# Moving matmul operands by 32 bytes in SBUF: stationary operands 32 bytes behind the moving ones, modulo 128

## The chip, the cores and the metric

The kernel runs on one core of one Trainium2 chip. The metric is the device time of one execution in microseconds. TensorE (PE) does the matmuls; a weight load (PEld, LDWEIGHTS) brings the stationary operand into the array, and the matmul then streams the moving operand past it. VectorE (DVE), ScalarE (ACT) and GpSimd (POOL) do the elementwise work, and SyncE (SP) issues most of the DMAs. SBUF is the on-chip memory; a tile's address is its byte offset within a partition.

## The reference

One decoder layer on a sequence of 2048 tokens and a model width of 1024, all in float32:

```python
def reference(x, ...):
    h = _rms(x, norm_mix_g[l])
    x = x + _mixer(h, ...)            # z = h @ w_in + b_in, three kinds of heads, y @ w_out
    h = _rms(x, norm_ffn_g[l])
    x = x + _conv_glu(h, ...)
    return x

def _conv_glu(h, w_up, conv_w, conv_b, w_down):
    u = _causal_dwconv(h @ w_up, conv_w) + conv_b
    gate, up = jnp.split(u, 2, axis=-1)
    return (jax.nn.silu(gate) * up) @ w_down
```

The mixer splits z into columns for eight attention heads with a forget gate, four mLSTM heads and four HGRN2 heads. w_in is 1024 x 3600, w_up 1024 x 5632, w_down 2816 x 1024.

## The kernel before

Every large product is done three times over in float32r: each operand is split into a high part and the rest, and high x high, high x rest and rest x high are summed in PSUM (`mm3`, L161). A split is a ScalarE copy and a subtraction on GpSimd or VectorE.

**Stages.** First the input projection, in two halves of 1024 tokens. `z_norm` (L169) normalises and transposes x into `hhi` and `hlo`, 128 partitions of the contraction, eight steps (`DT`) of 512 tokens. `z_groups` (L184) then walks through 14 groups of 256 columns of w_in. `load_split` (L146) loads a group's weights and splits them into `whi` and `wlo`. In a `ct_group` (L194) the weights are stationary and 512 tokens of `hhi`/`hlo` move, so that the result comes out transposed. In a `nat_group` (L207) 128 tokens of `hhi`/`hlo` are stationary and the weights move, 256 columns wide, or 264 in the two gated groups, where gate columns ride along. The moving weights of contraction step i begin at `whi[:, i, :]`, so i times 1024 bytes into the tile, or i times 1056 in the gated groups. The second half's groups are merged with the recurrent mixers. Then comes attention (L771 to L799), the output projection (`phase_out`, L877) and the feed-forward part.

**Feed-forward.** The up projection (`ffn_up`, L1048) runs for each half of the tokens over 22 pairs of column blocks. It uses a Strassen form with seven products instead of eight 512-deep ones: each product streams a 512-wide block of the tokens (`b11`, `b21`, `b22` or a sum or difference `t1` to `t4`, each as high part `h` and rest `l`) past a 128 x 128 block of the weights or of sums of them (tiles `w`). These weights come from the pool `fw`, but for three blocks of the first pair, which `up_first` puts into `hpool` ahead of time. `t3` and `b22` lie in the pool `ffnx2`, the other token blocks in `ffnx`. The down projection (`ffn_down`, L1164) is of the same form with both operands in `fw`.

**Addresses.** Pools are stacked from the left end of SBUF upwards or, with `side="right"`, from the right end downwards, in the order in which they are opened, so an unused tile at the right place shifts all that is opened after it. Four such tiles exist: `pad` (32 bytes) among the constants on the left, `padr` (32 bytes) first on the right, `padz` (32 bytes) in the pool of the input projection, and `padf` (256 bytes) in `ffnx`. With them the moving and the stationary operand of each matmul of the up, down, output and ungated input projections begin at the same address modulo 128 (64, in all of these).

The order of instructions is set by a scheduler when the kernel is built, except in the down projection, where it is written out.

Of the kernel before, what the change touches and what calls it, by code (L numbers as in the profile page):

```python
# [9 lines left out]
F32 = mybir.dt.float32  # L10
F32R = mybir.dt.float32r
# [9 lines left out]
P = 128  # L21
T = 2048
D = 1024
DT = D // P
# [118 lines left out]
        nc.vector.tensor_tensor(lo[:, 4 * q : 4 * q + 4, tok : tok + P], ps, h.bitcast(F32), op=ALU.subtract)  # L143


def load_split(k, wp, src, tag="w", n=2):  # L146

    nc = k.nc
    width = src.shape[1]
    hi = k.t(wp, [P, DT, width], F32R, tag=tag + "hi")  # L150
    lo = k.t(wp, [P, DT, width], F32R, tag=tag + "lo")
    for q in range(0, DT, n):
        raw = k.t(wp, [P, n, width], tag=tag + "raw")
        nc.sync.dma_start(raw, src[q * P : (q + n) * P, :].rearrange("(dt p) c -> p dt c", p=P))
        h = hi[:, q : q + n, :]
        nc.scalar.activation(h, raw, AF.Copy)  # L156
        nc.gpsimd.tensor_tensor(lo[:, q : q + n, :], raw, h.bitcast(F32), op=ALU.subtract)  # L157
    return hi, lo


def mm3(nc, out, lhs, rhs, n, lsl, rsl):  # L161


    for i in range(n):
        for j, (a, b) in enumerate(((0, 0), (0, 1), (1, 0))):
            nc.tensor.matmul(out, lsl(lhs[a], i), rsl(rhs[b], i), start=(i == 0 and j == 0), stop=(i == n - 1 and j == 2))  # L166
# [17 lines left out]
def z_groups(k, hf, pz, wp, psum, xbufs):  # L184
# [4 lines left out]
    w_in, b_in = k.a["w_in"][0], k.a["b_in"][0]  # L189
# [3 lines left out]

    def ct_group(off, dst, r0, c):  # L194

        w = load_split(k, wp, w_in[:, off : off + 256], n=4)
        for b in range(2):
            for ct in range(2):
                ps = k.t(psum, [P, BLK], tag="w")
                mm3(nc, ps, w, hts[b], DT, lambda x, i: x[:, i, ct * P : (ct + 1) * P], lambda x, i: x[:, i, :])  # L200
                st = k.t(pz, [P, BLK], tag="z", bufs=3)
                nc.scalar.activation(st, ps, AF.Identity, bias=k.col[:, c + ct : c + ct + 1])
                t0 = hf * HALF + b * BLK
                nc.scalar.dma_start(dst[r0 + ct * P : r0 + (ct + 1) * P, t0 : t0 + BLK], st)
                yield ct == 1
# [733 lines left out]
def h_tiles(k, fx, names):  # L939
    for n in names.split():  # L940
        k.hp[n] = tuple(fx.tile([P, 4, BLK], F32R, tag=n + x, name=n + x) for x in "hl")
# [378 lines left out]
def merge(main, side, rate):  # L1320

    due = 0.0
    for _ in main:
        due += rate
        while due >= 1.0:
            due -= 1.0
            if next(side, False) is False:
                due = 0.0
                break


def _trunk(ctx, tc, a, out):
    nc = tc.nc
    k = K(ctx, tc, a, out)

    def pool(stack, name, bufs, **kw):
        if kw.get("space") is not DRAM:
            kw["reuse_waits"] = "tile"
        return stack.enter_context(tc.tile_pool(name=name, bufs=bufs, **kw))

    dp = pool(ctx, "scratch", 1, space=DRAM)
    for name, shape in (
        ("s_qh", [512, T]),
        ("s_ql", [512, T]),
        ("s_kh", [512, T]),
        ("s_kl", [512, T]),
        ("s_v", [T, AH, 130]),
        ("s_fc", [AH, 2, T]),
        ("s_bqk", [512, T]),
        ("s_c", [512, T]),  # L1350
        ("s_n", [T, 1024]),
        ("s_rows", [NBLK, 28, BLK]),
        ("s_x2", [T, 1024]),
        ("s_h", [2, 2, 2, P, 4, BLK]),
        ("s_g", [2, 7, NP // 2, P, BLK]),
        ("s_w", [4, NP // 2, P, BLK]),
        ("s_one", [10, T]),
        ("s_y", [T, 1024]),
    ):
        setattr(k, name, dp.tile(shape, F32, tag=name, name=name))  # L1360
    cp = pool(ctx, "const", 1)
    k.ident = cp.tile([P, P], F32, tag="ident", name="ident")
    nc.scalar.dma_start(k.ident, a["ident"])
    k.halo = cp.tile([P, 2 * NP, 2], F32, tag="halo", name="halo")
    k.fcol = cp.tile([P, 4, 2 * NP], F32, tag="fcol", name="fcol")

    cp.tile([P, 8], F32, tag="pad", name="pad")
    pool(ctx, "pad", 1, side="right").tile([P, 8], F32, tag="padr", name="padr")

    with ExitStack() as ms:  # L1370
        cm = pool(ms, "cmix", 1)

        def mconst(name, shape, dt=F32, src=None):
            t = cm.tile(list(shape), dt, tag=name, name=name)
            if src is not None:
                nc.sync.dma_start(t, src)
            return t

        bc = ExitStack()
        pb = pool(bc, "bc", 1, side="right")  # L1380
        psb = pool(bc, "psb", 3, space=PSUM, side="right")
        k.q2 = pb.tile([P, 4, 2, P], F32, tag="q2", name="q2")
        nc.gpsimd.memset(k.q2, 0.0)
        with ExitStack() as zs:
            pz = pool(zs, "z", 2)
            wp = pool(zs, "w", 2)
            psw = pool(zs, "psw", 3, space=PSUM)
            k.gmix = pz.tile([P, D], F32, tag="gmix", name="gmix", bufs=1)
            xb, xw = ((pb, "v", 2), (pb, "p4", 2)), ((wp, "wraw", 2),)
            z = z_groups(k, 0, pz, wp, psw, (xb, xb))  # L1390
            next(z)
            pz.tile([P, 8], F32, tag="padz", name="padz", bufs=1)
            state(k, mconst)
            for _ in range(ZC):
                next(z)
            consts(k, a, cp, mconst, pz, psw, cm)
            mix = mixers(k, pb, psb)
            for _ in z:
                pass
            merge(z_groups(k, 1, pz, wp, psw, (xb, xw)), mix, RZ)  # L1400
        with ExitStack() as at:

            k.pat = {n: pool(at, "at_" + n, 1) for n in ("ga", "oT", "B0", "B1", "A0", "A1", "V1", "o1")}
            pa = pool(at, "att", 2)
            k.pat.update((n, pool(at, "at_" + n, 1)) for n in ("o0", "V0"))
            psa = pool(at, "psa", 2, space=PSUM)
            k.ga = k.pat["ga"].tile([P, 512], F32, tag="ga", name="ga", bufs=1)
            nc.sync.dma_start(k.ga, a["out_g"][0:1, 0:512].broadcast_to([P, 512]))
            att = attention(k, pa, psa)
            for _ in mix:  # L1410
                for _ in range(RA):
                    next(att, None)
            bc.close()
            wo = ExitStack()
            wor = ExitStack()
            w = w_out_load(k, pool(wo, "wo", 1, side="right"), pool(wor, "wor", 1, side="right"))
            for _ in att:
                pass

    wor.close()  # L1420
    py = pool(wo, "y", 2, side="right")
    psy = pool(wo, "psy", 1, space=PSUM, side="right")
    fx = pool(ctx, "ffnx", 1)

    fx.tile([P, 64], F32, tag="padf", name="padf")
    k.hp = {}
    h_tiles(k, fx, "b11 b21 t1 t2 t4")
    k.hpool = pool(ctx, "hpool", 10)
    with ExitStack() as os_:
        po = pool(os_, "po", 2)  # L1430
        k.gffn = po.tile([P, D], F32, tag="gffn", name="gffn", bufs=1)
        nc.sync.dma_start(k.gffn, a["norm_ffn_g"][0:1, :].broadcast_to([P, D]))
        pst = pool(os_, "pst", 2, space=PSUM)
        pso = pool(os_, "pso", 2, space=PSUM)
        psz = pool(os_, "psz", 1, space=PSUM)
        phase_out(k, w, py, (psy, psz), po, (psy, pso), pst)
    wo.close()
    fw = pool(ctx, "fw", 23, side="right")
    fx2 = pool(ctx, "ffnx2", 1, side="right")
    h_tiles(k, fx2, "t3 b22")  # L1440

    psp = [pool(ctx, f"psp{i}", 1, space=PSUM) for i in range(4)]
    k.psp = [psp[i] for i in (2, 3, 1, 0)]
    first = up_first(k)()
    h_parts(k, 0, 1)
    for hf in range(2):
        ffn_up(k, hf, fw, first)
        first = ffn_down(k, hf, fw)
# [19 lines left out]
def state(k, mconst):  # L1468

    nc = k.nc  # L1470
    k.half = mconst("half", [P, 1])
    nc.vector.memset(k.half, 0.5)

    sc = mconst("scan", [36, BLK])
    k.scan1 = k.scanc = sc
    nc.vector.memset(sc, 1.0)
    nc.vector.memset(sc.rearrange("p (c l) -> p c l", l=P)[32:36, :, 0:1], 0.0)
    k.carry = mconst("carry", [AH, 3])
    nc.vector.memset(k.carry, 0.0)
    nc.vector.memset(k.carry[:, 2:3], NEG)  # L1480
    k.bstate = mconst("bstate", [P, 2, 2, 65])
    nc.vector.memset(k.bstate, 0.0)
    k.cstate = mconst("cstate", [P, 2, HD])
    nc.vector.memset(k.cstate, 0.0)
# [105 lines left out]
```

## Time and profile before

| | us |
|---|---|
| median of 3 runs | 2980.77 (2980.37 to 2982.65) |
| profiled execution, its own time | 2982.74 |
| its span, first to last instruction | 2981.0 |
| PE busy | 2834.5 (95%) |
| PE weight loads busy | 2350.0 (79%) |
| DVE / ACT / POOL busy | 2055.0 / 1255.0 / 1412.5 |
| mean granted PE clock | 0.975 of full speed |

A group's line in the profile gives the source line, the engine, the operation, the tiles written and read, the shape, the number of instructions, their busy time in us, the mean of one in ns, and the idle time before them. A matmul's busy time runs on while the next one has already begun, so how fast a stream goes is read from the starts on the timeline and not from the length of one matmul: in the up projection a matmul is 389 ns long, and the next begins 227 ns after it. Matmul rows name the moving operand first and the stationary one second, and the weight load's rows are a group of their own (PEld).

### The profile page before, as it was taken

The page shows a single profiled execution, that of the slowest core. Times are in us where ns is not written, and L with a number is a line of the kernel's source. Part 1 is how long each engine was busy: PE and PEld are TensorE (multiplying, and loading weights), DVE is VectorE, ACT ScalarE, POOL GpSimd, SP SyncE. Part 2 cuts the span into 40 slices and gives each one's busy share as a digit, 9 for nine tenths or more (in the row PEclk, how much of TensorE's full clock was granted, in tenths as well). Part 3 has the DMA queues.
Part 4 walks back from the last instruction along what each step waited for, and adds up shares of the span by engine and source line. Part 5 has one row for each costly group of instructions (what it writes and reads, how often), then busy time and mean ns, then how long its engine had stood idle before and what let it go on. Part 6 is the DMA issues. An engine that isn't in the chain of part 4 may idle for free. (4 is left out here: it accounts for less than half of the span.)

```text
span 2981.0 us, 43125 instructions
## 1 busy us (share of the span) xinstructions
PE 2834.5 (95%) x15181; PEld 2350.0 (79%) x15181; DVE 2055.0 (69%) x3637; ACT 1255.0 (42%) x2138; POOL 1412.5 (47%) x1149
## 2 busy tenths in 40 slices
PE   7999999899978988899999999999999999999999
PEld 7889989899766665566688778888878888888887
DVE  6426688757379886777746567777697677777655
ACT  3232332312225456677623344444454344444443
POOL 2233434643245556756501176666476544444443
PEclk9999999999988889999999999999999999999999
DMA  5333434433261334433056634544677433333666
GB/s 170 115 113 123 148 106 128 144 93 94 93 149 49 77 66 97 100 71 66 18 182 212 198 129 163 161 157 155 222 263 260 155 105 105 100 102 124 226 206 214
DMA packets 332025, 406.88 MB, mean 136 GB/s; under 512 B 31010, under 2 KB 219504, under 8 KB 328640
## 3 DMA queue, kind: packets, MB, share of 16 engines
q1 hardware_dynamic: 296192, 335.37, 37.5%
q10 hardware_dynamic: 33264, 60.37, 5.4%
q0 software_dynamic: 2352, 8.39, 1.0%
q8 instruction: 119, 1.95, 0.3%
q14 instruction: 98, 0.80, 0.1%
HBM read 276.05 MB, written 127.98 MB: 136 GB/s over the span
## 5 line engine op out<-in xcount | busy, mean ns | idle before, releaser
L1027 POOL TENSOR_TENSOR w<-w,w 128x512 fp32r<-128x512 f32 x302 | 405.0, 1354 | 400.2 <-ACT w L1026 286.1
L1215 PE MATMUL ps<-w,w 128*128 128x512 f32 x1848 | 421.2, 390 | 4.4 <-ACT w L1206 1.9
L1215 PEld LDWEIGHTS ps<-w,w 128*128 128x128 f32 x1848 | 346.6, 188 | 78.2 <-POOL w L1208 2.6
L166 PE MATMUL w<-whi,hhi 128*128 128x256 f32 (+1 forms) x1280 | 369.4, 289 | 2.1 <-DVE pg L228 1.5
L166 PE MATMUL w<-wlo,hhi 128*128 128x256 f32 (+1 forms) x1280 | 367.7, 288 | 0.6 <-POOL wlo L157 0.6
L166 PE MATMUL w<-whi,hlo 128*128 128x256 f32 (+1 forms) x1280 | 367.0, 287 | 0.0
L783 POOL TENSOR_TENSOR pl<-pf,ph 128x512 fp32r<-128x512 f32 (+1 forms) x224 | 269.3, 1214 | 175.6 <-ACT ph L780 113.0
L1208 POOL TENSOR_TENSOR w<-w,w 128x512 fp32r<-128x512 f32 x154 | 215.4, 1405 | 204.4 <-ACT w L1206 172.3
L1026 ACT ACTIVATE w<-w 128x512 fp32r<-128x512 f32 x302 | 180.7, 627 | 261.0 <-POOL w L1027 82.5
L1207 DVE TENSOR_TENSOR w<-w,w 128x512 fp32r<-128x512 f32 x154 | 180.5, 1182 | 104.7 <-ACT w L1205 103.2
L166 PEld LDWEIGHTS w<-whi,hhi 128*128 128x128 f32 x1280 | 246.9, 193 | 3.7 <-issue 2.0
L166 PEld LDWEIGHTS w<-wlo,hhi 128*128 128x128 f32 x1280 | 246.7, 193 | 1.8 <-POOL wlo L157 1.0
L166 PEld LDWEIGHTS w<-whi,hlo 128*128 128x128 f32 x1280 | 246.4, 193 | 0.2
L745 DVE TENSOR_REDUCE mx<-m 128x1 f32<-128x512 f32 (+2 forms) x320 | 188.3, 604 | 63.6 <-PE m L740 36.2
L778 ACT ACTIVATE pf<-s 128x512 f32<-128x512 f32 (+1 forms) x320 | 168.4, 539 | 144.1 <-DVE pl L783 49.9
L157 POOL TENSOR_TENSOR wlo<-wraw,whi 128x1024 fp32r<-128x1024 f32 (+1 forms) x56 | 137.9, 2483 | 170.6 <-ACT whi L156 167.7
L1032 DVE TENSOR_TENSOR w<-w,w 128x512 f32<-128x512 f32 x176 | 151.2, 878 | 81.5 <-DMA w<-in_w_up_dram 69.4
L780 ACT ACTIVATE ph<-pf 128x512 fp32r<-128x512 f32 (+1 forms) x320 | 178.1, 575 | 45.8 <-PE pv L798 38.5
L1073 DVE SCALAR_TENSOR_TENSOR u<-ps,fcol,u 128x1023 f32<-128x1023 f32 x88 | 108.9, 1278 | 91.6 <-ACT u L1072 91.6
L771 PE MATMUL s<-QB,KB 70*128 70x512 f32 (+1 forms) x320 | 134.1, 419 | 30.7 <-ACT pf L778 30.3
L740 PE MATMUL m<-KB,QB 70*128 70x512 f32 (+2 forms) x320 | 135.3, 438 | 21.1 <-DVE mx L745 12.4
L1206 ACT ACTIVATE w<-w 128x512 fp32r<-128x512 f32 x154 | 96.7, 628 | 114.3 <-PE ps L1215 89.5
(349 smaller groups left out, 7102.1 us busy)
## 6 DMA issues: line engine op xcount, KB each, us to landing
w<-in_w_up_dram SPq DMA_DIRECT2D x182, 256.0 KB
w<-s_g SPq DMA_DIRECT2D x154, 256.0 KB
w<-in_w_down_dram SPq DMA_DIRECT2D x110, 256.0 KB
wraw<-in_w_in_dram SPq DMA_DIRECT2D x48, 512.0 KB
s_g<-u ACTq DMA_DIRECT2D x88, 256.0 KB
w<-s_w SPq DMA_DIRECT2D x88, 256.0 KB
s_g<-w ACTq DMA_DIRECT2D x66, 256.0 KB
w<-s_h SPq DMA_DIRECT2D x48, 256.0 KB
```

The source lines that it names most:

```text
L157: nc.gpsimd.tensor_tensor(lo[:, q : q + n, :], raw, h.bitcast(F32), op=ALU.subtract)
L166: nc.tensor.matmul(out, lsl(lhs[a], i), rsl(rhs[b], i), start=(i == 0 and j == 0), stop=(i == n - 1 and j == 2))
L745: nc.vector.tensor_reduce(mx[:, i, kb : kb + 1], ps[:, 0:n], axis=AX.X, op=ALU.max)
L778: nc.scalar.activation(pf[:, c0:], ps[:, c0:], AF.Exp)
L780: nc.scalar.activation(ph[:, c0:], pf[:, c0:], AF.Copy)
L783: eng.tensor_tensor(pl[:, c0:], pf[:, c0:], ph[:, c0:].bitcast(F32), op=ALU.subtract)
L1026: nc.scalar.activation(h, t, AF.Copy)
L1027: nc.gpsimd.tensor_tensor(lo, t, h.bitcast(F32), op=ALU.subtract)
L1032: nc.vector.tensor_tensor(t, x, y, op=op)
L1207: nc.vector.tensor_tensor(gl, gr, gh.bitcast(F32), op=ALU.subtract)
L1208: nc.gpsimd.tensor_tensor(wl, wr, wh.bitcast(F32), op=ALU.subtract)
L1215: nc.tensor.matmul(tiles[tile], g[x][:, tile * P : (tile + 1) * P], w[y], start=j == 0 and c == 0, stop=j == nj - 1 and c == 2,)
```

## The change

The change only moves tiles in SBUF. `pad` and `padz` go, `padr` grows from 32 to 64 bytes, `padf` shrinks from 256 to 224, and `load_split` gets a parameter `off`, a number of float32 elements left free at the front of `whi` and `wlo`; `ct_group` passes 16 (64 bytes).

```diff
-def load_split(k, wp, src, tag="w", n=2):
+def load_split(k, wp, src, tag="w", n=2, off=0):
...
-    hi = k.t(wp, [P, DT, width], F32R, tag=tag + "hi")
-    lo = k.t(wp, [P, DT, width], F32R, tag=tag + "lo")
+    hi, lo = (
+        k.t(wp, [P, off + DT * width], F32R, tag=tag + x)[:, off:].rearrange("p (a c) -> p a c", c=width)
+        for x in ("hi", "lo")
+    )
...
-        w = load_split(k, wp, w_in[:, off : off + 256], n=4)
+        w = load_split(k, wp, w_in[:, off : off + 256], n=4, off=16)
...
-
-    cp.tile([P, 8], F32, tag="pad", name="pad")
-    pool(ctx, "pad", 1, side="right").tile([P, 8], F32, tag="padr", name="padr")
+    pool(ctx, "pad", 1, side="right").tile([P, 16], F32, tag="padr", name="padr")
...
-            pz.tile([P, 8], F32, tag="padz", name="padz", bufs=1)
...
-    fx.tile([P, 64], F32, tag="padf", name="padf")
+    fx.tile([P, 56], F32, tag="padf", name="padf")
```

The addresses modulo 128 that follow, worked out from the tiles' places in the built program, and the offset stationary minus moving:

| matmuls | stationary, moving before | offset | stationary, moving after | offset |
|---|---|---|---|---|
| input, nat groups, 256 wide | `hhi` 64, `whi` 64 | 0 | `hhi` 32, `whi` 0 | 32 |
| input, gated nat groups, 264 wide | `hhi` 64, `whi` 64 + 32i | 0, 96, 64, 32 in turn | `hhi` 32, `whi` 32i | 32, 0, 96, 64 in turn |
| input, ct groups, 512 wide | `whi` 64, `hhi` 64 | 0 | `whi` 64, `hhi` 32 | 32 |
| up, with b11, b21, t1, t2, t4 | `w` 64, `b11` 64 | 0 | `w` 32, `b11` 0 | 32 |
| up, first pair's blocks from `hpool` | 64, 64 | 0 | 0, 0 | 0 |
| up, with t3, b22 | 64, 64 | 0 | 32, 32 | 0 |
| down | 64, 64 | 0 | 32, 32 | 0 |

The output projection and attention keep their offsets; the transposes get other ones. All offsets of 32 are 32 modulo 256, too. The order of the instructions on each engine is the same before and after. One thing beside addresses differs: `t3`'s high part now begins 32 bytes lower against the output stage's pool and so reaches 32 bytes into its second `x2` buffer, and ScalarE's first write to it waits for that buffer as well.

## The prediction

> **What bounds the kernel now.** I read the page's busy line and clock line first, then the chain, then the busy time by stage, then single matmuls on the timeline. The page:
>
> ```profile
> PE 2834.5 (95%) x15181; PEld 2350.0 (79%) x15181; DVE 2055.0 (69%) x3637; ACT 1255.0 (42%) x2138; POOL 1412.5 (47%) x1149
> PE ps L1058 25%; PE ps L1215 12%; PE w L166 1%; DMA w<-in_w_up_dram 1%; POOL w L1027 1%; DVE w L1032 1%; DVE u L1074 0%; POOL w L1208 0%; DVE w L965 0%; DMA w<-in_w_down_dram 0%; DVE u L1073 0%; DMA s_g<-w 0%; DMA w<-s_g 0%; PE tn L911 0%; ACT u L1072 0%
> ```
>
> TensorE is the bound, and in the part of the chain that the page follows the up projection (L1058) is the largest piece. The chain does not reach back to the input projection, so that stage has to be judged by its busy time. Stages below, as us, PE, PEld, DVE, ACT, POOL, clock, DMA: the two halves of the input projection (the second with the mixers beside it), attention, and the long stretches of the up projection in each half.
>
> ```profile
> 0.00:409.00 409.00, 384.60 (x2760) 363.02 (x2761) 235.44 (x642) 132.35 (x195) 127.90 (x123) 0.99 0.41 132
> 409.00:821.00 412.00, 393.83 (x2849) 364.92 (x2850) 274.02 (x640) 118.28 (x193) 168.34 (x165) 0.99 0.35 109
> 821.00:1480.00 659.00, 580.19 (x2985) 405.42 (x2984) 515.72 (x997) 381.66 (x746) 386.99 (x322) 0.91 0.35 78
> 1738.00:2123.00 385.00, 384.50 (x1696) 317.84 (x1695) 273.96 (x320) 167.96 (x266) 246.94 (x183) 1.00 0.49 161
> 2377.00:2760.00 383.00, 381.96 (x1681) 315.25 (x1682) 299.58 (x402) 157.67 (x219) 175.19 (x136) 1.00 0.33 106
> ```
>
> PE is busy 94% and 96% of the two input stages and over 99% of the up stretches, at full clock. So what counts is how far apart two matmuls start. One 512-wide and one 256-wide stream from the timeline (start us, length us), and a piece of the 256-wide stream in a window that the windows view gives as clock 0.50:
>
> ```profile
> 32.40:34.00 1.60, 1.60 (x9) 1.60 (x9) 1.56 (x5) 0.58 (x1) 0.00 (x0) 0.50 0.05 13
> ```
>
> ```profile
> 32.37 0.42 PE L166 MATMUL w<-wlo,hhi 128*128 128x256 f32 x1
> 34.08 0.41 PE L166 MATMUL w<-whi,hhi 128*128 128x256 f32 x1
> ...
> 38.74 0.28 PE L166 MATMUL w<-wlo,hhi 128*128 128x256 f32 x1
> 40.18 0.28 PE L166 MATMUL w<-wlo,hhi 128*128 128x256 f32 x1
> ...
> 1800.97 0.39 PE L1058 MATMUL ps<-t2h,w 128*128 128x512 f32 x1
> 1803.69 0.39 PE L1058 MATMUL ps<-t4h,w 128*128 128x512 f32 x1
> ```
>
> At half clock eight starts lie in 1.71 us, 214 ns for 256 columns; at full clock the columns alone would then take 107 ns, and 512 columns 213 ns. At full clock twelve 256-wide starts take 1.44 us (120.0 ns each), and twelve 512-wide ones 2.72 us (226.7 ns each). Both lose the same 13.3 ns per matmul over their columns, so the loss goes with the matmul, or with its weight load, and not with the columns. That loss is all that placement can touch.
>
> **The change part by part.** The instructions stand in the same order on every engine before and after; what differs are addresses. I count by the two addresses of each matmul, stationary minus moving, modulo 128 bytes. Before, the offset is 0 in the up projection, in the input projection's 256-wide and 512-wide groups, in the down projection and in the output projection. After, it is 32 in the 3,072 256-wide matmuls (1,024 of each of three kinds), in the 768 512-wide ones of the transposed groups (256 of each kind), and in 2,568 of the 3,696 of the up projection: 1,056 with t3 or b22 stay at 0, and so do 72 of the first column block, whose weights lie in another pool (3,696 − 1,056 − 72). Groups by form:
>
> ```profile
> L166 PE MATMUL w<-whi,hhi 128*128 128x256 f32 x1024 | 295.3, 289 | 0.6 <-ACT hhi L142 0.6
> L166 PE MATMUL w<-hhi,whi 128*128 128x512 f32 x256 | 101.8, 398 | 1.2 <-ACT z L202 1.2
> L1058 PE MATMUL ps<-b11h,w 128*128 128x512 f32 x352 | 117.0, 393 | 2.2 <-DVE u L1079 1.5 <-ACT halo L1076 0.5
> L1215 PE MATMUL ps<-w,w 128*128 128x512 f32 x1848 | 421.2, 390 | 4.4 <-ACT w L1206 1.9 <-POOL w L1208 1.5 <-ACT halo L1076 1.0
> ```
>
> So 6,408 matmuls are touched. On the path I count the 2,568 of the up projection whole, and nine tenths of the 3,840 of the input projection (PE's 94% and 96% there, less some for the mixers that share the stage): 3,456; together 6,024. Each nanosecond is 6.0 us, and 0.2% of the time, about the least that a measurement of this kernel can tell from no change, is 6 us: one nanosecond per matmul.
>
> The price of offset 32 stands nowhere as a steady stream, but the gated groups bound it. Their weight rows are 264 columns, 1,056 bytes, so the moving address steps 32 bytes modulo 128 with each of the eight contraction steps while the stationary one stays. The offset runs 0, 96, 64, 32, 0, 96, 64, 32 over steps of three matmuls. Starts of the first matmul of each step, one whole cycle:
>
> ```profile
> 105.73 0.28 PE L166 MATMUL w<-whi,hhi 128*128 128x264 f32 x1
> ...
> 106.09 0.28 PE L166 MATMUL w<-whi,hhi 128*128 128x264 f32 x1
> ...
> 106.45 0.29 PE L166 MATMUL w<-whi,hhi 128*128 128x264 f32 x1
> ...
> 106.82 0.28 PE L166 MATMUL w<-whi,hhi 128*128 128x264 f32 x1
> ...
> 107.17 0.28 PE L166 MATMUL w<-whi,hhi 128*128 128x264 f32 x1
> ...
> 107.53 0.28 PE L166 MATMUL w<-whi,hhi 128*128 128x264 f32 x1
> ...
> 107.90 0.28 PE L166 MATMUL w<-whi,hhi 128*128 128x264 f32 x1
> ...
> 108.26 0.29 PE L166 MATMUL w<-whi,hhi 128*128 128x264 f32 x1
> ...
> 108.63 0.28 PE L166 MATMUL w<-whi,hhi 128*128 128x264 f32 x1
> ```
>
> 264 columns are 110 ns by the same rate, 0.33 us a step. The steps take 0.36, 0.36, 0.37, 0.35, 0.36, 0.37, 0.36, 0.37 us. The two steps at offset 32 are the shortest and one of the longest: losses of 6.7 and 13.3 ns per matmul. The two at offset 0 lose 10 ns each, less than the steady 13.3 at the same offset, so three matmuls are too few to settle, and these rows give bounds rather than a price. The whole cycle is 2.90 us, 120.8 ns each, a loss of 10.8. That is the value I take for a steady offset 32, as the mean over all offsets, since the two direct readings lie on either side of it (mean 10.0). The saving is 13.3 − 10.8 = 2.5 ns; 6,024 × 2.5 ns = 15.1 us.
>
> The ends: the best step (6.7) saves 6.6 ns, 40 us; losing nothing at all would save 13.3 ns, 80 us. Upwards, a 512-wide stream at offset 0 that has just been interrupted runs slower before it settles:
>
> ```profile
> 1738.84 0.40 PE L1058 MATMUL ps<-t3h,w 128*128 128x512 f32 x1
> ...
> 1740.00 0.62 PE L1058 MATMUL ps<-t3h,w 128*128 128x512 f32 x2
> ```
>
> Five starts lie in 1.16 us, 232 ns each: 5.3 ns worse than settled. If offset 32 held the stream in such a state, that would be +32 us.
>
> Two weight loads of the same shape show that a load next to a wide moving stream is longer than one next to a 128-wide one, which speaks for the two reads meeting:
>
> ```profile
> L1215 PEld LDWEIGHTS ps<-w,w 128*128 128x128 f32 x1848 | 346.6, 188 | 78.2 <-POOL w L1208 2.6 <-ACT w L1206 2.4 <-ACT halo L1076 1.4
> L892 PEld LDWEIGHTS ty<-ident,yin 128*128 128x128 f32 x128 | 14.6, 141 | 2.5 <-DVE nrs L120 1.5 <-issue 0.2
> ```
>
> [...]
>
> Transposes also get new offsets (L892 64 to 32, L911 0 to 64). In the chain of waits:
>
> ```profile
> 1656.57 0.87 PE tn L911 x8
> 1657.45 0.87 PE ty L892 x8
> ```
>
> Eight take 0.87 us at offset 0 and eight at 64 take the same, so I cost them at nothing.
>
> ScalarE's first split into t3h now overlaps by 32 bytes a buffer of the output stage that it did not touch, and waits for that buffer's readers too. Queued behind it there is the split into b22h, which already waits for the last transposed tile's store:
>
> ```profile
> 1706.06 0.63 ACT L946 ACTIVATE t3h<-w 128x512 fp32r<-128x512 f32 x1
> 1708.23 0.63 ACT L946 ACTIVATE b22h<-w 128x512 fp32r<-128x512 f32 x1 [1.54 <-DMA s_h<-pc]
> ```
>
> The new wait is for earlier work than that, so it can cost between nothing and the 2.2 us between the rows; I take 0.5. VectorE's split of t3 waits for it, and the up projection's product with t3 for that. The removed and added pads issue nothing.
>
> Sum: −15.1 + 0.5 = −14.6 us. The profiled execution took 2982.7 us (its span 2981.0 and 1.7 around it), so 2968.1; it lies 2.0 above the median 2980.8 of the runs shown, so the forecast for the median is 2966.
>
> **The rivals.**
> A. Placement matters more than the mean says: steady offset 32 is the good step, 6.7 ns or less. For it: one direct step shows it, and a constant offset has no bad step to recover from. Against: the other direct step. 2982.7 − 40 − 2.0 gives 2941; without any loss 2901. [...]
> B. No change: the loss is a fixed cost per weight load that no offset moves, as the equal 13.3 ns at both widths suggests, or steady offset 32 also loses 13.3, as the second direct step does. The time would be 2981, and the change would not do what it says. [...]
> C. Slower: at offset 32 load and stream meet for longer, and the stream no longer settles. The place is the same 6,024 matmuls; the price is up to 5.3 ns, 32 us, 3013; at the half of it 2997. It decides from 14.3 ns of loss per matmul, 1 ns over today's. For it: the second step at offset 32 is already at the settled value, where offset 0 in the same rows is 3.3 ns below its own settled value; add those 3.3 and a settled offset 32 would lose 16.6 ns, 3001. Against: the first step.
>
> **How the numbers follow.** My case has 0.30, A 0.22, B 0.20, C 0.28. The point is my case, 2966. Its own range is 2956 to 2975 (1 to 4 ns saved). For 8 in 10 I take in A down to 2925, which leaves out only the losses near nothing (0.08), and C up to 2999 (leaving 0.10). Faster by over 0.2% is my case and A, 0.52; within, 0.20; slower, 0.28.
>
> **What would show it.** In the changed kernel's timeline twelve 512-wide starts of t1, t2, t4, b11 or b21 should take 2.69 us instead of 2.72 and twelve 256-wide ones 1.41 instead of 1.44, while t3, b22 and the down projection stay at 2.72. Right so far, but the stage windows no shorter, would mean that the matmuls were not the bound in the input projection. The weight load's mean of 188 ns should fall if the two reads meet less. The forecast is wrong if the touched starts stay within 1 ns of today's, or lengthen.

## The result, and the profile after

The change is slower. The median of six runs is 3000.73 us (2995.91 to 3001.28) against 2982.48 us (2980.37 to 2985.61) of six runs of the kernel before on the same chip: a ratio of 1.0058, with a 95% interval of 1.0045 to 1.0071. The profiled execution took 3001.28 us. That is 35 us above the point forecast and just past the upper end of the range; of the cases, it is rival C.

The page's busy line, and the same four stretches as before (us, PE, PEld, DVE, ACT, POOL, clock, DMA share, GB/s, with the number of instructions in brackets):

```profile
PE 2856.5 (95%) x15181; PEld 2348.4 (78%) x15181; DVE 2053.8 (68%) x3637; ACT 1255.6 (42%) x2138; POOL 1414.4 (47%) x1149
```

```profile
0.00:409.00 409.00, 384.58 (x2765) 360.89 (x2766) 236.35 (x646) 132.65 (x195) 128.10 (x123) 0.99 0.41 132
409.00:821.00 412.00, 397.49 (x2850) 365.62 (x2849) 274.08 (x637) 118.67 (x193) 169.90 (x166) 0.98 0.35 110
1738.00:2123.00 385.00, 384.61 (x1657) 310.86 (x1656) 265.69 (x314) 161.45 (x257) 239.67 (x178) 1.00 0.48 157
2377.00:2760.00 383.00, 381.41 (x1644) 308.23 (x1643) 292.62 (x391) 155.81 (x216) 178.63 (x139) 1.00 0.31 99
```

Busy time is the wrong number to read here: PE is as busy as before in both up stretches. The count in the brackets tells it. The same 385 us at the same full clock hold 1,657 matmuls instead of 1,696, and the same 383 us hold 1,644 instead of 1,681. At 227 ns each, 39 and 37 missing matmuls are 8.9 and 8.4 us: 17.3 of the 18.3 us lie there. In the first half of the input projection the count went up by 5, in the second by 1.

The starts show why. A 512-wide stream of t2 (at offset 32), its neighbour t4 (at 32) and b22 (which stayed at 0), and then a 256-wide stream of the input projection:

```profile
1801.14 0.40 PE L1061 MATMUL ps<-t2h,w 128*128 128x512 f32 x1
...
1803.94 0.40 PE L1061 MATMUL ps<-t4h,w 128*128 128x512 f32 x1
...
1806.74 0.39 PE L1061 MATMUL ps<-b22h,w 128*128 128x512 f32 x1
...
1809.48 0.40 PE L1061 MATMUL ps<-b21h,w 128*128 128x512 f32 x1
```

```profile
63.00 0.28 PE L169 MATMUL w<-wlo,hhi 128*128 128x256 f32 x1
...
64.42 0.28 PE L169 MATMUL w<-wlo,hhi 128*128 128x256 f32 x1
```

Twelve starts at offset 32 take 2.80 us, 233.3 ns each, where they took 2.72; twelve of b22 take 2.74, because each product at offset 0 now follows one at 32 and has to settle again: the first five spacings of t3 and b22 are 228 to 235 ns on average, the later ones 226.7. Twelve 256-wide starts take 1.42 us, 118.3 ns each, against 1.44. So the same offset slows the wide matmuls and speeds up the narrow ones.

The groups say it more weakly, since a matmul's length is not its spacing: the 256-wide group fell from 289 to 287 ns, the 512-wide one of the input projection rose from 398 to 402, b11's from 393 to 397, and the down projection, still at offset 0, kept its 390 or so:

```profile
L169 PE MATMUL w<-whi,hhi 128*128 128x256 f32 x1024 | 293.1, 287 | 0.6 <-ACT hhi L142 0.6
L169 PE MATMUL w<-hhi,whi 128*128 128x512 f32 x256 | 102.9, 402 | 0.2 <-ACT z L205 0.2
L1061 PE MATMUL ps<-b11h,w 128*128 128x512 f32 x352 | 118.4, 397 | 2.0 <-DVE u L1082 1.5 <-ACT halo L1079 0.4
L1218 PE MATMUL ps<-w,w 128*128 128x512 f32 x1848 | 423.9, 391 | 3.5 <-ACT w L1209 2.0 <-POOL w L1211 0.8 <-ACT halo L1079 0.7
```

The mean spacing over all starts that follow one another directly at full clock, worked out from the two traces:

| matmuls | before, ns | after, ns |
|---|---|---|
| input, 256 wide | 119.75 (offset 0) | 118.27 (offset 32) |
| input, 512 wide | 227.19 (0) | 233.28 (32) |
| up, with b11, b21, t1, t2, t4 | 226.77 (0) | 233.39 (32) |
| up, with t3, b22 | 226.77 (0) | 228.62 (0) |
| down | 226.74 (0) | 226.77 (0) |

From these, 3,072 x −1.5 ns, 2,568 x 6.6, 768 x 6.1 and 1,056 x 1.85 are −4.6, +16.9, +4.7 and +2.0 us: +19.0, against 18.3 measured.

### The profile page after: what moved, and what is told of

It reads as the page before. It is cut to its first block, busy times and chain, and to the rows that moved or that the text cites. A ratio compares the mean times of both kernels' runs of the same rounds, so it can differ in the third digit from the quotient of the medians.

```text
span 2999.5 us, 43127 instructions
## 1 busy us (share of the span) xinstructions
PE 2856.5 (95%) x15181; PEld 2348.4 (78%) x15181; DVE 2053.8 (68%) x3637; ACT 1255.6 (42%) x2138; POOL 1414.4 (47%) x1149
## 5 line engine op out<-in xcount | busy, mean ns | idle before, releaser
L1209 ACT ACTIVATE w<-w 128x512 fp32r<-128x512 f32 x154 | 97.0, 630 | 113.3 <-PE ps L1218 89.1
```

## The experiments

**1. Streams alone.** Is this TensorE with its two operands, or does the rest of the kernel take part? Each entry of the kernel's list is one stream at chosen addresses:

```diff
+        for i in range(cnt):
+            s = i % 8
+            nc.tensor.matmul(acc[0:wc, 0:n],
+                wt[:, w // 4 + s * 128 : w // 4 + s * 128 + wc],
+                mv[:, m // 4 + s * 512 : m // 4 + s * 512 + n], ...)
```

> This kernel leaves out the whole trunk: it only runs separate streams of 48 float32r matmuls, each with its own weight load, on one PSUM bank, with no other work beside them; widths 512, 384, 256 and 128, and for each width stationary operands that start 0, 4, 8, 16, 32, 48, 64, 80, 96, 112, 128 or 160 bytes behind the moving ones, a few of them again at other absolute addresses, and with 64 or 32 stationary columns. Theory 1 (each width and offset has its own settled spacing, a matter of TensorE and its two operands alone): 512 wide 226.7 ns from start to start at offset 0 and 128, 233.3 ns at 32 and 160; 256 wide about 119.8 ns at 0 and 117 to 118.3 ns at 32; the same at any absolute address with the same offset. Rival 1 (the absolute address of one operand decides): streams with both operands at 32, 64 or 96 differ from those with both at 0. Rival 2 (the spacing comes from other engines' and queues' traffic in the SBUF): all offsets of one width come out equal here, and under 226.7 ns at 512.

Mean spacing in the second half of each stream (ns), worked out from the starts in the trace:

| offset, bytes | 0 | 8 | 32 | 64 | 96 | 128 | 160 |
|---|---|---|---|---|---|---|---|
| 512 columns | 226.67 | 230.75 | 233.33 | 233.33 | 234.25 | 232.08 | 233.33 |
| 384 columns | 173.33 | 173.29 | 173.33 | 174.71 | 173.33 | 176.00 | 176.67 |
| 256 columns | 120.00 | 115.54 | 118.33 | 113.33 | 118.75 | 120.00 | 120.00 |
| 128 columns | 111.67 | 111.67 | 111.67 | 111.67 | 111.67 | 111.67 | 111.67 |

With nothing else in the machine the streams show the values of the kernel's up and down projections to 0.1 ns and those at 256 columns to 0.3 ns (only the input projection's 227.19 ns at 512 columns lies 0.5 ns over), so rival 2 falls. Both operands at 32, 64 or 96 give 226.67 and 120.00 again, so rival 1 falls at steps of 32 bytes. (With the moving operand at 16 and the stationary one at 48 the wide stream took 226.67 ns although the offset is 32, so finer placement counts.) Two things were not expected: 128 differs from 0 at 512 columns, so the change's "modulo 128" is not the period, and 256 columns have a far better offset, 64.

**2 to 4. The parts of the change by themselves.** All three beside the same kernel before (2986.40 us median there).

```diff
-    fx.tile([P, 64], F32, tag="padf", name="padf")
+    fx.tile([P, 56], F32, tag="padf", name="padf")
```

> Only the up projection is changed: the pad ahead of its moving tiles is 56 instead of 64 floats, so 2,556 or so of its 512-wide matmuls have their weights 32 bytes behind, and t3 and b22 stay at offset 0; the input projection is as before. Theory 1 (own settled spacing of each width and offset): 233.4 against 226.8 ns on 2,568 matmuls is +16.9 us, and the offset-0 products that resettle behind them +1.9 us: about 18.8 us slower than before. Rival 1 (what I forecast, one price per matmul at both widths): 2.5 ns less on 2,568, 6.4 us faster. Rival 2 (the products lose only while both offsets alternate with the input projection's traffic, or the loss is elsewhere): within 3 us of before.

Measured: 2996.38 us, ratio 1.0040 (1.0028 to 1.0052), 8 to 16 us slower. The stretches of the up projection look like those of the change, 1,659 and 1,644 matmuls, and the spacings are 233.39 ns at 32 and 228.54 for t3 and b22:

```profile
1738.00:2123.00 385.00, 384.86 (x1659) 311.08 (x1658) 272.42 (x313) 161.72 (x254) 237.18 (x179) 1.00 0.49 158
2377.00:2760.00 383.00, 381.36 (x1644) 308.14 (x1643) 295.38 (x394) 153.47 (x214) 173.66 (x135) 1.00 0.32 103
```

Both rivals fall. In the times the loss is less than the 18.8 us of theory 1, and the interval leaves that out. The traces show how far the stage bears it out: from its first matmul's start to its last one's, both halves together, the up projection took 899.2 us here, and 898.4 to 900.8 in the three other traces with this offset; where it is not touched it took 881.9 in the trace of before and 884.5, 885.4 and 886.7 in those of experiments 3, 4 and 6. So the stage is 12 to 19 us longer, 14.7 on average. Half clock does not account for what is missing: the runs' granted clocks are alike, 0.977 on average here and 0.976 in the 23 runs of before, and over those 23 a step of 0.001 goes with 1.4 us. Why the stage shows less than the 18.8 us of spacing is not settled.

For the 512-wide groups of the input projection alone, `load_split` gets its `off` and

```diff
-        w = load_split(k, wp, w_in[:, off : off + 256], n=4)
+        w = load_split(k, wp, w_in[:, off : off + 256], n=4, off=8)
```

> Only the column-major groups of the input projection are changed (768 matmuls of 512 columns): stationary operands at 96, moving ones at 64 modulo 128, so offset 32 at another absolute address than in the change (64 and 32). Theory 1: 233.3 against 227.2 ns, 736 of them back to back, is +4.5 us. Rival 1 (the absolute address decides): no loss, within 1 us of before. Rival 2 (one price at both widths, my forecast): 2.5 ns less each, 1.9 us faster.

Measured: 2986.39 us, ratio 1.0009 (0.9998 to 1.0020), which leaves out rival 2 and does not tell theory 1 from rival 1. The trace does: 233.30 ns over 739 starts, at another absolute address than in the change, so rival 1 falls. The input projection, from its first matmul's start to its last one's, took 808.4 us against 806.1, half of what theory 1 adds up; the same stage untouched took 804.9 in experiment 2, so such a time is good to about 1 us. The group's row stands at the change's value, 401 ns against 398 before:

```profile
L168 PE MATMUL w<-hhi,whi 128*128 128x512 f32 x256 | 102.6, 401 | 0.3 <-ACT z L204 0.3
```

For the 256-wide groups alone, `padz` goes, and the `off=8` holds the 512-wide ones at offset 0:

```diff
-            pz.tile([P, 8], F32, tag="padz", name="padz", bufs=1)
```

> Only the row-major groups of 256 columns are changed (3,072 matmuls, offset 32); the 512-wide groups and the up projection stay at offset 0. Theory 1: 118.27 against 119.75 ns is -4.6 us. Rival 1 (my forecast's price of 2.5 ns each): -7.7 us. Rival 2 (the 256-wide streams do not set the end, or the faster spacing is a matter of their neighbours): within 1 us of before.

Measured: 2981.96 us, ratio 0.9987 (0.9975 to 0.9999), 0.3 to 7.5 us faster; 118.30 ns over 2,820 starts; the input projection took 801.0 us against 806.1. So the narrow part of the change is a gain, and its spacing is that of theory 1, 1.45 ns less and not rival 1's 2.5. The interval of the times just leaves out rival 1's 7.7 us and just touches rival 2; the 5.1 us of the stage are against rival 2.

**5. The real address patterns, in steps of 32 bytes.** The streams now have the order and strides of the kernel's own groups:

```diff
+def nat(g):
+    return [(2048 * i + 512 * g + 16384 * x, 1024 * i + 8704 * y)
+            for i in range(8) for x, y in ((0, 0), (0, 1), (1, 0))]
```

> This kernel leaves out the whole trunk: it runs streams of 72 float32r matmuls alone, in the order and with the strides of the addresses that the kernel's own groups have (row-major input groups of 256 columns, column-major ones of 512, up projection, down projection), and moves one operand against the other in steps of 32 bytes over 512 to 1,024 bytes. The first streams gave 113.3 ns for 256 columns at offset 64 against 120.0 at 0, and 226.7 at 0 against 233.3 at 32 and 232.1 at 128 for 512 columns. Theory 1 (the address difference alone sets the spacing a stream settles in, not modulo 128 but over a longer period): at 256 columns some offset gives 113.3 ns again, at 512 columns 0 is the best or nearly so with 226.7 and the others lie at 228 to 235. Rival 1 (period 128): the values at d, d+128, d+256 and d+384 are equal within 0.5 ns. Rival 2 (chance of the start decides which spacing a stream settles in): with the real strides the fast 113.3 ns at offset 64 is gone, and no pattern in the offset shows.

The timeline shows a whole stream of 72 as one row: start, length. The 256-wide ones at offsets 0, 32, 64, and the 512-wide ones of the up projection at 0, 32, 128, 256:

```profile
36.40 8.90 PE L195 MATMUL nat_m_w<-mv,wt 128*128 128x256 f32 x72 [0.78 <-DVE res L201]
45.82 8.78 PE L195 MATMUL nat_m_w<-mv,wt 128*128 128x256 f32 x72 [0.52 <-DVE res L201]
55.11 8.44 PE L195 MATMUL nat_m_w<-mv,wt 128*128 128x256 f32 x72 [0.52 <-DVE res L201]
```

```profile
471.76 16.61 PE L195 MATMUL up_m_w<-mv,wt 128*128 128x512 f32 x72 [0.52 <-DVE res L201]
489.16 17.07 PE L195 MATMUL up_m_w<-mv,wt 128*128 128x512 f32 x72 [0.78 <-DVE res L201]
...
542.77 17.00 PE L195 MATMUL up_m_w<-mv,wt 128*128 128x512 f32 x72 [0.78 <-DVE res L201]
...
613.82 16.66 PE L195 MATMUL up_m_w<-mv,wt 128*128 128x512 f32 x72 [0.79 <-DVE res L201]
```

At 512 columns 32 loses 0.46 us in 71 spacings, 128 loses 0.39, and 256 is back at 0's value. Settled, the offsets 0, 32, ..., 224 give 226.67, 233.33, 233.33, 234.17, 232.39, 233.33, 228.89, 233.33 ns, and with the stationary operand moved they repeat every 256 bytes within 0.2 ns up to 1,024; the patterns of the column-major groups and of the down projection give the same but for offset 128 or 384 (232.4 or 233.3). At 256 columns: 120.00, 118.31, 113.33, 117.42, 118.69, 120.00, 117.78, 117.78 in steps of 32, repeating likewise. The difference alone is not all, though: where the moving operand was shifted instead, 192 of 256 gave 113.33 and 64 gave 117.78 once and 113.33 once. So in these streams theory 1 holds with a period of 256 where the stationary operand moves, and rivals 1 and 2 fall; the next experiment brings rival 2 back.

**6. The kernel with the good offset for each width.** Nothing of the change, one new edit: the narrow groups' weights start 48 elements further in, so that the offset is 64.

```diff
-        w = load_split(k, wp, w_in[:, off : off + width], n=4)
+        w = load_split(k, wp, w_in[:, off : off + width], n=4, off=0 if gated else 48)
```

> The kernel before with one edit: the weights' tiles of the row-major groups of 256 columns start 192 bytes further in, so that the stationary operand lies 64 bytes behind the moving one modulo 256 in 3,072 matmuls; all 512-wide matmuls stay at offset 0. Theory 1 (a stream settles in the spacing that its operands' address difference modulo 256 gives, as the streams alone showed: 113.33 ns at 64 against 120.00 at 0): 3,072 x -6.4 ns is -19.7 us, and some less where the stream is broken: about 18 us faster than before. Rival 1 (in the kernel other engines' traffic keeps the stream from settling there): 117 to 120 ns and at most 8 us faster. Rival 2 (the input projection is not PE's to set here: the loads and splits of the next weights end last once the matmuls take less): idle time before its matmuls grows by what the spacing saves, and the gain stays under 10 us.

Measured: 2974.49 us against 2984.24 us of before beside it, ratio 0.9967 (0.9952 to 0.9981): 6 to 14 us faster, and the fastest of all versions here. An undisturbed stream runs as the scan said, twelve starts in 1.36 us, 113.3 ns each:

```profile
87.66 0.28 PE L168 MATMUL w<-whi,hlo 128*128 128x256 f32 x1
...
89.02 0.28 PE L168 MATMUL w<-whi,hlo 128*128 128x256 f32 x1
```

Over all 2,816 starts the mean is 115.65 ns, and the starts in the trace show why. Of the 59 unbroken streams of 19 or more matmuls at full clock, 33 ran at 113.3 ns past their sixth spacing and 26 at about 117.8; none went over from one to the other before it was interrupted. In 12 products of 24 matmuls, which have one PSUM tile, one pair of weight tiles and one block of tokens, both occur, on either side of an interruption. Here transposes (L319) break into one after its fourth matmul: twelve starts take 1.36 us before, most of them in the product ahead of it with the same weights, and 1.41 us after:

```profile
308.45 0.28 PE L168 MATMUL w<-whi,hlo 128*128 128x256 f32 x1
...
309.81 0.28 PE L168 MATMUL w<-whi,hlo 128*128 128x256 f32 x1
...
310.04 0.60 PE L319 MATMUL t<-ident,z 128*128 128x128 f32 x4
...
311.07 0.28 PE L168 MATMUL w<-whi,hhi 128*128 128x256 f32 x1
...
312.48 0.28 PE L168 MATMUL w<-whi,hhi 128*128 128x256 f32 x1
```

So the offset of 64 does not fix the spacing by itself: after an interruption a stream settles in one of two, as rival 2 of experiment 5 had it. What decides between them is not shown. The slow starts after an interruption count for little: the first six spacings average 116.6 ns, the others 115.45. All starts together save 2,816 x 4.1 = 11.5 us of spacing, and the input projection took 798.1 us against 806.1, 8 us less. So the 18 us that I expected were too many: theory 1's spacing is there in about half of the streams; why the other 3.5 us of spacing do not show in the stage is not settled. Rival 1 would have kept all streams above 117 ns and falls. PE's idle time before the first group's matmuls is 0.6 us as before, against rival 2.

**7. What collides.** Addresses that alternate from matmul to matmul, finer steps, and narrower stationary operands:

```diff
+def own(d):   # a matmul's own difference kept, the next stationary one's against this moving one's swings
+    return lambda g: [(512 * (i % 8) + d * (i % 2), 2048 * (i % 8) + d * (i % 2)) for i in range(24)]
+def nxt(d):   # the other way round
+    return lambda g: [(512 * (i % 8) + d * ((i + 1) % 2), 2048 * (i % 8) + d * (i % 2)) for i in range(24)]
```

> This kernel leaves out the whole trunk: streams of 48 to 72 float32r matmuls alone. In the first ten kinds both operands' addresses alternate from matmul to matmul, so that either the difference of a matmul's own two operands, or the difference of the next matmul's stationary operand and this one's moving operand, stays at the good value (0 for 512 columns, 64 for 256) while the other swings by 32 to 192 bytes. Theory 1a (what collides is the load of the next weights with the moving operand that is streaming): streams with the next difference kept stay at 226.7 and 113.3 ns, those with only the own difference kept go to 228 to 235 and 115 to 120 ns. Theory 1b (a matmul's own two operands collide): the other way round. Rival (neither; absolute addresses or the order): both change or none does. The rest of the streams move the stationary operand in steps of 4 bytes over 256 (expected: no 512-wide stream under 226.7 ns), move the moving operand to 16 modulo 32, take 264 columns with a row of 1,056 bytes as in the gated groups (expected 120.9 ns at any offset) and of 1,280 bytes (expected 116.7 ns at the best offset, 110 + 6.7), and narrow the stationary operand from 128 to 8 columns (expected, if the load's length makes the loss: the loss over the columns' time shrinks with it).

The first two alternating streams, own kept and next kept, with swings of 32 bytes at 512 columns; both are near the 17.07 us of a steady offset 32 and not the 16.61 of 0:

```profile
36.60 17.09 PE L329 MATMUL s_own_alt<-mv,wt 128*128 128x512 f32 x72 [0.78 <-DVE res L335]
54.48 17.01 PE L329 MATMUL s_next_alt<-mv,wt 128*128 128x512 f32 x72 [0.79 <-DVE res L335]
```

Over all swings the settled spacing is 228.3 to 234.0 ns with the own difference kept and 230.0 to 232.2 with the next one kept; at 256 columns 116.7 to 120.0 and 116.7 to 120.0. So neither 1a nor 1b holds, as the rival said: keeping one difference is not enough. Whether both differences count, or the alternation of the addresses itself, these streams do not tell apart. In steps of 4 bytes, and with the moving operand at 16, there is no smooth curve: of 80 streams of 512 columns 35 settle at 233.33 and 9 at 226.67, none below; of 80 of 256 columns 18 settle at 120.00, 10 at 118.33, 9 at 116.67 and 6 at 113.33, none below. With both operands at 16 the streams took 230.00 and 118.33 ns, not offset 0's 226.67 and 120.00, so at this finer step the absolute address counts, too. And 512 columns at offset 16 took 233.3 ns in experiment 1 and 226.67 here. Two expectations missed. Rows of 1,280 bytes for 264 columns gave 120.0 to 126.7 ns, never 116.7 (1,056 bytes: 120.6 to 122.6). And the loss does not shrink with the load: with 8 stationary columns 512 moving ones still take 226.67 ns at offset 0, 228.92 at 32 and 231.67 at 64. In between, offset 0 is no longer good: 230.00 ns with 96 or 64 stationary columns and 231.67 with 32 (experiment 1 has the same for 64 and 32). The length of the weight load is not what is lost (loads of 64 and 32 columns took 121 ns on average in experiment 1, those of 128 took 189), but its width changes the spacing at offset 0.

**8 and 9. The change again, and all its wide matmuls without the narrow ones.** The ninth kernel has the edits of 2 and 3 together.

> The change itself once more, beside the next kernel on the same chip. Theory 1 (each width settles by its own: 512 columns lose 6.6 ns at offset 32, 256 columns gain 1.5): 18 us slower than before, as first measured. Its stretch of the up projection from 1738 to 2123 us holds some 38 matmuls fewer than before's 1,696.

> All 512-wide matmuls that the change touches at offset 32 (2,568 of the up projection and 768 of the input projection), the 256-wide ones left at offset 0. Theory 1: 2,568 x 6.6 + 768 x 6.1 ns is 21.6 us, and 1.9 us for the offset-0 products that resettle: about 23 us slower than before, and some 4 us slower than the change. Rival 1 (the parts do not add; the up projection alone measured 12 us in the times, not 19): 12 to 16 us slower, less than the change.

Measured beside one kernel before (2983.74 us): the change 2998.10 us, ratio 1.0051 (1.0039 to 1.0063); the wide part alone 3000.87 us, ratio 1.0062 (1.0048 to 1.0075). As the medians go, the wide part costs all of the change's loss and 3 us more, which the narrow part gives back; the spacings are 233.39 and 233.31 ns at 512 columns, 119.74 at 256. The interval reaches from 14 to 22 us, so it touches rival 1's upper end, with theory 1's 23 just outside; that the wide part alone costs more than the change is against that rival, though only by the medians, since the two intervals overlap. The change's own stretch:

```profile
1738.00:2123.00 385.00, 384.69 (x1658) 310.77 (x1657) 273.67 (x314) 161.95 (x255) 236.81 (x178) 1.00 0.49 159
```

## Why the prediction was wrong

**What bounds the kernel: right in kind, not shown to the nanosecond.** Both stages grew or shrank with the spacing of their matmuls. The up projection became 12 to 19 us longer for 18.9 us of spacing (16.9 + 2.0). The input projection gave back 2.3 us of 4.5, 5.1 of 4.6 and 8.0 of 11.5 in experiments 3, 4 and 6, where a time of this stage is good to about 1 us; the nine tenths that I took lie among these.

**"The loss goes with the matmul, and not with the columns": the step that failed.** It rested on 13.3 ns at both widths at offset 0. At that offset it holds: 384 columns, 160 ns by the same rate, lose 13.3 as well. At other offsets it does not. At 32 the loss over the columns is 11.6 ns at 256, 13.3 at 384 and 20.0 at 512; at 64 it is 6.7, 14.7 and 20.0. With one price for both widths I could not see that the change would gain on 3,072 matmuls and lose on 3,336.

**The price of 10.8 ns: mis-sized, and with the wrong sign where it counts.** It was the mean of a 264-wide stream whose offset changes every three matmuls. The streams at a steady offset settled in spacings of their own (alone, at 256 columns, 120.00 ns at offset 0, 118.33 at 32, 113.33 at 64), so neither the mean nor single steps bounded the price. Nor were the steps what I read them as: with the period of 256 of experiment 5, the two at offset 32 modulo 128 were one at 32 and one at 160, and the two at 0 one at 0 and one at 128. The term of −15.1 us was −4.6 us on the narrow matmuls and +21.6 us on the wide ones. I said that three matmuls are too few to settle, and then took their mean for a settled value.

**The upper bound of 5.3 ns: close, and one nanosecond too low.** The 232 ns of a disturbed 512-wide stream were the one row of the same width, and the settled value at 32 is 233.4, 6.6 over before. Rival C had the stream not settle any more. It does settle, at that size: in the products with t4 the spacings go to and fro between 231.6 and 234.5 ns from the second on. C's 3001 us was met by luck, by its time and not by its price: it took 16.6 ns of loss for every matmul, and the measured losses are 20.0 and 11.6.

**The 1,056 that stay at offset 0: a term left out.** I cost t3 and b22 at nothing. They resettle after each neighbour at 32 and lose 1.85 ns, 2.0 us.

**The wait for t3h: nothing instead of 0.5 us.** ScalarE's two splits start as before:

```profile
1705.92 0.63 ACT L949 ACTIVATE t3h<-w 128x512 fp32r<-128x512 f32 x1
1708.40 0.64 ACT L949 ACTIVATE b22h<-w 128x512 fp32r<-128x512 f32 x1 [1.84 <-DMA s_h<-pc]
```

**Transposes: right.** Eight still take 0.87 us at their new offsets:

```profile
1656.15 0.87 PE tn L914 x8
1657.02 0.87 PE ty L895 x8
```

**The weight load's length as a sign: wrong.** It did not move while the stream slowed by 6.6 ns a matmul: 189 ns before and 188 after for b11, 188 both times for t3, which stayed at offset 0. So the 188 against 141 ns did not speak for a collision; the two streams differ in width, 512 and 128 columns. After:

```profile
L1061 PEld LDWEIGHTS ps<-b11h,w 128*128 128x128 f32 x352 | 66.2, 188 | 19.1 <-issue 2.4 <-ACT halo L1079 0.8 <-ACT w L1029 0.3
L1061 PEld LDWEIGHTS ps<-t3h,w 128*128 128x128 f32 x352 | 66.3, 188 | 14.8
```

**Open:** how the addresses come to set the spacings. Shown is that the addresses of both operands set them without any other engine (alone, at 512 columns, 226.67 ns at offset 0 and 233.33 at 32), that neither a matmul's own difference nor the next one's decides alone (228.3 to 234.0 and 230.0 to 232.2 ns with the one or the other kept at 0), that the load's width does not scale the loss (226.67 ns at offset 0 with 128 stationary columns and with 8), and that a narrow stream at offset 64 can settle in either of two spacings (113.3 and about 117.8 ns).

## What to carry to other kernels

The streams of 256 and of 512 columns here settled in spacings that depended on their width and on where their two operands lay, so an offset that is good for one width may be bad for another (alone, 32 instead of 0 took 512 columns from 226.67 to 233.33 ns and 256 from 120.00 to 118.33): measure it for each width as a steady stream, alone, with the kernel's own strides, and don't take it from a stream whose offset changes. To see such a loss in a profile, count instructions in equal windows or twelve starts on the timeline; busy shares did not move (384.50 us of 385 with 1,696 matmuls before, 384.61 with 1,657 after). A gain found in streams alone was an upper bound here (6.67 ns at offset 64 alone, 4.1 in the kernel), because the kernel breaks its streams and they settled now at 113.3 ns, now at about 117.8: look at them one by one, and not only at their mean.

## What the runs showed of the hardware

At half clock the loss is gone: in the trace of before, 512-wide matmuls that follow one another at a granted clock of 0.50 start 426.7 ns apart (mean of 23) and 256-wide ones 213 (median of 21), so twice the columns take twice the time with nothing added. At full clock no stream of 512 columns settled under 226.67 ns, 13.3 over half of the 426.7, which is the estimate here of what its columns alone take. All streams here load weights for each matmul (15,181 loads and as many matmuls in the trace of before, 3,472 of each in experiment 1).

The settled spacings gather at a few values: 49 of the 80 streams of 512 columns in experiment 7 lie at 226.67, 230.00 or 233.33, and 43 of the 80 of 256 at 113.33, 116.67, 118.33 or 120.00. A step of 4 bytes can be enough to leave one: 48 matmuls of 512 columns took 11.19 us at offset 0 and 11.43 at 4 in experiment 1. At 128 columns twelve offsets all gave 111.67 ns.

The time spent at half clock differs from one profiled execution to another, 134 to 156 us in the eight of whole kernels here, most of it in the attention stage (113 of 152 us in the trace of before). That is a spread of the same size as the smaller effects, and the reason why a part worth 5 us had to be read from the trace and not from the times.
